# Two steps of mixing work in a row between the dense products of a hybrid encoder layer

## The chip, the cores and the metric

The kernel runs on one core of a Trainium2 chip. The metric is the device time of one execution in microseconds. The median of three runs of the kernel before is 2088.24 us (2086.25 to 2090.12).

## What is computed

One encoder layer with shared weights for two requests, a prompt of 512 tokens (`p`) and a sample of 1024 (`s`), all in float32 with a model width of 1024:

```
h    = rmsnorm(x)
proj = h @ w_in                       # 4096 columns: q, two gates, values, gate of HGRN; q, k, v of attention
o_h  = HGRN2 forward + HGRN2 backward # 4 heads of 128, gated linear recurrence, in chunks
o_a  = neighbourhood attention        # 8 heads of 64 on a grid 64 wide, windows of 8 x 16
x    = x + concat(o_h, o_a) @ w_out
x    = x + (silu(rmsnorm(x) @ w_gate) * (rmsnorm(x) @ w_up)) @ w_down
```

## The kernel before

The dense products (input projection, output projection, FFN) are made on TensorE from operands split into a high and a low part, three products for each block (lines 167 to 169 and 180 to 182, line 922 in the last stages). Each weight block is loaded by SyncE's queue, cast by ScalarE (line 109) and its rest taken by VectorE (line 110).

The mixing (HGRN and attention, and the norms) is written as Python generators, each cut into *steps* by `yield`. A step gives a few instructions to each engine. `queue` holds generators that wait, `active` those that have begun, up to a window. `micro()` takes one step of the active generator whose turn it is. Between the dense products stand calls of `quantum()`: one after every six dense matmuls. It adds `rate` to a credit, and takes one step for each whole credit. So the rate sets how densely mixing is strewn into dense work; `finish()` takes what is left at the end of a stage.

The list of units at the end of `trunk` sets the order of the work around the change:

- the prompt's first projections, with the norms as mixing (rate 1.8, window 2), up to some 80 us;
- the prompt's HGRN heads (rate 0.75, window 2), up to about 252 us;
- the sample's first projections with the prompt's attention as mixing (rate 1.8, window 6), up to about 430 us;
- the sample's HGRN heads (rate 0.75, window 2), up to about 757 us;
- the prompt's output projection and gate and up products, with the sample's attention as mixing (rate 1.8, window 4), up to about 1188 us;
- then the sample's output projection and FFN, without such mixing.

An HGRN head's work on one half of 512 tokens is `half_mix`: a step that makes the tiles (no TensorE work), one of block products of queries with key sums (`blocks`, line 311: eight matmuls, 16 in the profile's count, into PSUM tiles of 64 x 64), seven steps of levels, then the transposes of the keys (line 372) and the state products (line 379). A level makes eight block products from `kh` and `QQ` (line 311), scales the keys (line 330, VectorE) and copies them in another order (line 299, ScalarE), and rewrites both halves of `QQ` (lines 339 and 342, VectorE) for the next level. So a level can begin only when VectorE has rewritten `QQ` behind the block products of the level before. `out_half` then has three steps: output products (line 446), norm on VectorE, transposes (line 462).

The code is not the last word on the order. The framework's scheduler takes the instructions with the program's order as their priority, and sets each engine's order by when it holds the inputs of an instruction to be ready, and by when buffers are free.

Of the kernel before, what the change touches and what calls it, by code (L numbers as in the profile page):

```python
# [46 lines left out]
def trunk(ctx, tc, x_p, x_s, nmw, w_in, lbw, gnw, qnw, knw, rpb, w_out, nfw, w_g, w_u, w_d,  # L47
# [106 lines left out]
    def mm_nat(xT, ts, ws, done):  # L154


        pss = {}
        for s, slot in enumerate(ws):
            w = slot.rearrange("p h (k c) -> p h k c", k=2)
            for t in ts:  # L160
                if s == 0:
                    pss[t] = dense_ps()
                ps = pss[t]
                for j in range(2):
                    k = 2 * s + j
                    xh, xl = (xT[t // 4][i][:, k, t % 4 * 128:t % 4 * 128 + 128] for i in range(2))
                    pe.matmul(ps, lhsT=xh, rhs=w[:, 0, j, :], start=k == 0, stop=False)  # L167
                    pe.matmul(ps, lhsT=xh, rhs=w[:, 1, j, :], start=False, stop=False)  # L168
                    pe.matmul(ps, lhsT=xl, rhs=w[:, 0, j, :], start=False, stop=k == NK - 1)  # L169
                if s == len(ws) - 1:  # L170
                    done(t, ps)
                quantum()

    def mm_tr(ps, xT, w, t0=0, n=512):

        wv = w.rearrange("p h (k c) -> p h k c", k=NK)
        ts = slice(t0, t0 + n)
        for k in range(NK):
            xh, xl = xT[0][:, k, ts], xT[1][:, k, ts]
            pe.matmul(ps[:, ts], lhsT=wv[:, 0, k, :], rhs=xh, start=k == 0, stop=False)  # L180
            pe.matmul(ps[:, ts], lhsT=wv[:, 0, k, :], rhs=xl, start=False, stop=False)  # L181
            pe.matmul(ps[:, ts], lhsT=wv[:, 1, k, :], rhs=xh, start=False, stop=k == NK - 1)  # L182
            if k % 2 == 1:
                quantum()
# [3 lines left out]
    mix = {"rate": 0.0, "credit": 0.0, "window": 2}  # L188
    active, queue = [], []

    def micro():
        while True:
            while queue and len(active) < mix["window"] and queue[0][0]():
                active.append(queue.pop(0)[1]())
            if not active:
                return False
            g = active.pop(0)
            try:
                next(g)
            except StopIteration:  # L200
                continue
            active.append(g)
            return True

    def quantum():
        mix["credit"] += mix["rate"]
        while mix["credit"] >= 1:
            mix["credit"] -= 1
            if not micro():
                mix["credit"] = 0  # L210

    norms = {}

# [1067 lines left out]
```

## Time and profile before

| what | value |
| --- | --- |
| median of three runs | 2088.24 us |
| the profiled execution, its time | 2091.29 us |
| its span, first to last instruction | 2089.5 us |
| busy: TensorE, its weight loads | 1996.0 us, 1598.9 us |
| busy: VectorE, ScalarE, GpSimd | 1231.8 us, 812.1 us, 379.9 us |
| mean granted TensorE clock | 0.984 |

Busy time is the union of an engine's instructions. Ends of matmuls are modelled, and matmuls overlap, so a row of the timeline that says 0.39 us doesn't mean that the next cannot start for so long: the distance between starts is what counts. In a timeline, "PE" is TensorE's matmuls, "PEld" its weight loads, "DVE" VectorE, "ACT" ScalarE; a row may hold several instructions (xN).

### The profile page before, as it was taken

The page shows a single profiled execution, that of the slowest core. Times are in us where ns is not written, and L with a number is a line of the kernel's source. Part 1 is how long each engine was busy: PE and PEld are TensorE (multiplying, and loading weights), DVE is VectorE, ACT ScalarE, POOL GpSimd, SP SyncE. Part 2 cuts the span into 40 slices and gives each one's busy share as a digit, 9 for nine tenths or more (in the row PEclk, how much of TensorE's full clock was granted, in tenths as well). Part 3 has the DMA queues.
Part 4 walks back from the last instruction along what each step waited for, and adds up shares of the span by engine and source line. Part 5 has one row for each costly group of instructions (what it writes and reads, how often), then busy time and mean ns, then how long its engine had stood idle before and what let it go on. Part 6 is the DMA issues. An engine that isn't in the chain of part 4 may idle for free. (4 is left out here: it accounts for less than half of the span.)

```text
span 2089.5 us, 28456 instructions
## 1 busy us (share of the span) xinstructions
PE 1996.0 (96%) x10546; PEld 1598.9 (77%) x10546; DVE 1231.8 (59%) x2489; ACT 812.1 (39%) x1457; POOL 379.9 (18%) x310
## 2 busy tenths in 40 slices
PE   7999999999999999999999895899999998999999
PEld 5777887778788877778778784677777776887887
DVE  7677534576766667665654237656556554556644
ACT  5545335543433445555552224233223222323332
POOL 1200000000000000011112103344444441244300
PEclk9999999999999999999999997899999999999999
DMA  7832463432122274444455521223232224755443
GB/s 229 258 102 76 128 207 108 132 92 86 41 72 86 61 225 138 115 137 136 133 156 165 211 76 35 72 100 96 91 116 96 91 94 144 253 172 176 139 138 117
DMA packets 236833, 266.54 MB, mean 128 GB/s; under 512 B 19653, under 2 KB 168155, under 8 KB 236439
## 3 DMA queue, kind: packets, MB, share of 16 engines
q1 hardware_dynamic: 191904, 192.59, 30.8%
q10 hardware_dynamic: 41079, 61.27, 8.3%
q0 software_dynamic: 3712, 10.87, 1.7%
q8 instruction: 83, 1.36, 0.3%
q14 instruction: 55, 0.45, 0.1%
HBM read 194.84 MB, written 70.20 MB: 127 GB/s over the span
## 5 line engine op out<-in xcount | busy, mean ns | idle before, releaser
L110 DVE TENSOR_TENSOR w<-wst,w 128x1024 fp32r<-128x1024 f32 x128 | 157.1, 1229 | 147.9 <-ACT w L109 147.4
L109 ACT CAST w<-wst 128x1024 fp32r<-128x1024 f32 x128 | 134.1, 1048 | 175.2 <-PE pd L169 71.0
L922 PE MATMUL pd<-bo,ao 128*128 128x512 f32 x792 | 194.5, 393 | 4.6 <-ACT bo L916 4.6
L922 PEld LDWEIGHTS pd<-bo,ao 128*128 128x128 f32 x792 | 150.1, 190 | 36.6 <-ACT bo L916 5.0
L922 PE MATMUL pd<-opA,w 128*128 128x512 f32 x528 | 135.8, 400 | 18.0 <-ACT s L1036 10.8
L922 PE MATMUL pm<-bo,ao 128*128 128x512 f32 x594 | 147.9, 390 | 3.7 <-DVE bo L917 3.7
L922 PE MATMUL pd<-opS,w 128*128 128x512 f32 x528 | 135.9, 407 | 14.2 <-ACT opS L916 5.8
L182 PE MATMUL pd<-h2p,w 128*128 128x512 f32 (+1 forms) x368 | 143.0, 389 | 0.0
L180 PE MATMUL pd<-h2p,w 128*128 128x512 f32 (+1 forms) x368 | 142.5, 387 | 0.0
L181 PE MATMUL pd<-h2p,w 128*128 128x512 f32 (+1 forms) x368 | 142.1, 386 | 0.0
L922 PE MATMUL pm<-opS,w 128*128 128x512 f32 x528 | 135.4, 399 | 5.9 <-DVE sg L1018 4.7
L922 PEld LDWEIGHTS pd<-opA,w 128*128 128x128 f32 x528 | 99.1, 191 | 45.9 <-ACT s L1036 17.3
L922 PEld LDWEIGHTS pd<-opS,w 128*128 128x128 f32 x528 | 100.4, 194 | 43.1 <-DVE u L1044 11.4
L922 PEld LDWEIGHTS pm<-bo,ao 128*128 128x128 f32 x594 | 111.3, 188 | 27.9 <-DVE bo L917 5.0
L167 PE MATMUL pd<-w,hs 128*128 128x512 f32 x320 | 130.9, 409 | 0.0
L916 ACT CAST w<-wst 128x512 fp32r<-128x512 f32 x110 | 64.7, 617 | 166.0 <-POOL S L909 82.4
L169 PE MATMUL pd<-w,hs 128*128 128x512 f32 x320 | 126.4, 395 | 0.0
L168 PE MATMUL pd<-w,hs 128*128 128x512 f32 x320 | 126.0, 394 | 0.0
L922 PEld LDWEIGHTS pm<-opS,w 128*128 128x128 f32 x528 | 99.8, 192 | 32.1 <-DVE sg L1018 8.1
L917 DVE TENSOR_TENSOR w<-wst,w 128x512 fp32r<-128x512 f32 x110 | 89.3, 829 | 57.4 <-ACT w L916 57.3
L811 POOL DMA_DIRECT2D ost<-ot_p x8 | 4.3, 540 | 649.5 <-DMA pj_s<-ev 637.1
L917 DVE TENSOR_TENSOR ao<-wst,ao 128x768 fp32r<-128x768 f32 x77 | 88.6, 1155 | 8.4 <-ACT ao L916 6.8
(233 smaller groups left out, 4320.0 us busy)
## 6 DMA issues: line engine op xcount, KB each, us to landing
wst<-in_w_in_dram SPq DMA_DIRECT2D x68, 512.0 KB, 4.3
wst<-in_w_gate_dram SPq DMA_DIRECT2D x44, 512.0 KB, 3.9
wst<-in_w_up_dram SPq DMA_DIRECT2D x44, 512.0 KB, 4.3
wst<-g_S SPq DMA_DIRECT2D x44, 384.0 KB, 3.2
wst<-g_A SPq DMA_DIRECT2D x33, 384.0 KB, 3.7
g_S<-S ACTq DMA_DIRECT2D x44, 256.0 KB, 2.4
pj_s<-ev ACTq DMA_DIRECT2D x40, 256.0 KB, 2.4
bias<-bias_d SPq DMA_DIRECT2D x192, 48.0 KB, 2.0
```

The lines of the kernel that those rows point to most:

```text
L109: act.copy(out=w[:, 0, :], in_=s)
L110: dve.tensor_tensor(out=w[:, 1, :], in0=s, in1=f32(w[:, 0, :]), op=ALU.subtract)
L167: pe.matmul(ps, lhsT=xh, rhs=w[:, 0, j, :], start=k == 0, stop=False)
L168: pe.matmul(ps, lhsT=xh, rhs=w[:, 1, j, :], start=False, stop=False)
L169: pe.matmul(ps, lhsT=xl, rhs=w[:, 0, j, :], start=False, stop=k == NK - 1)
L180: pe.matmul(ps[:, ts], lhsT=wv[:, 0, k, :], rhs=xh, start=k == 0, stop=False)
L181: pe.matmul(ps[:, ts], lhsT=wv[:, 0, k, :], rhs=xl, start=False, stop=False)
L182: pe.matmul(ps[:, ts], lhsT=wv[:, 1, k, :], rhs=xh, start=False, stop=k == NK - 1)
L811: st.dma_start(out=s, in_=dram[b, "o", k][:, u * 512:u * 512 + 512])
L916: act.copy(out=dst[0], in_=src)
L917: dve.tensor_tensor(out=dst[1], in0=src, in1=f32(dst[0]), op=ALU.subtract)
L922: pe.matmul(ps, lhsT=l[a], rhs=r[b_], start=start and i == 0, stop=stop and i == 2, skip_group_check=more)
```

## The change

`quantum()` now does nothing until the credit has reached two, and then takes steps until less than one is left.

```diff
     def quantum():
         mix["credit"] += mix["rate"]
-        while mix["credit"] >= 1:
-            mix["credit"] -= 1
-            if not micro():
-                mix["credit"] = 0
+        if mix["credit"] >= 2:
+            while mix["credit"] >= 1:
+                mix["credit"] -= 1
+                if not micro():
+                    mix["credit"] = 0
```

Behind this place the changed program's lines have numbers higher by one: line 311 is 312 there, 372 is 373, 379 is 380.

How the order on TensorE moves is seen best in the sample's HGRN stretch. The first place is the end of the first half of the first head, where the second half begins. `KK` are the keys that are transposed, `q,ks` is the second half's first block product, `w,hs` are dense products. Before:

```order
L168 MATMUL pd<-w,hs_2564 128x512
L169 MATMUL pd<-w,hs_2565 128x512
L372 MATMUL pm<-ident,KK 128x128 x7
L167 MATMUL pd<-w,hs_2564 128x512
L168 MATMUL pd<-w,hs_2564 128x512
```

After the change:

```order
L168 MATMUL pd<-w,hs_2564 128x512
L169 MATMUL pd<-w,hs_2565 128x512
L373 MATMUL pm<-ident,KK 128x128 x7
L312 MATMUL pm<-q,ks 64x64 x8
L167 MATMUL pd<-w,hs_2564 128x512
L168 MATMUL pd<-w,hs_2564 128x512
```

Here two steps of different halves stand side by side; before, the block products came 24 dense products later, with the state products (L379) between.

The second place is a little further on, in the levels of that second half: two consecutive levels with the dense products between them. Before:

```order
L311 MATMUL pm<-QQ,kh 64x64 x8
L167 MATMUL pd<-w,hs_2564 128x512
L168 MATMUL pd<-w,hs_2564 128x512
L169 MATMUL pd<-w,hs_2565 128x512
L167 MATMUL pd<-w,hs_2564 128x512
L168 MATMUL pd<-w,hs_2564 128x512
L169 MATMUL pd<-w,hs_2565 128x512
L311 MATMUL pm<-QQ,kh 64x64 x8
```

After the change:

```order
L312 MATMUL pm<-QQ,kh 64x64 x8
L167 MATMUL pd<-w,hs_2564 128x512
L168 MATMUL pd<-w,hs_2564 128x512
L169 MATMUL pd<-w,hs_2565 128x512
L167 MATMUL pd<-w,hs_2564 128x512
L312 MATMUL pm<-QQ,kh 64x64 x8
L168 MATMUL pd<-w,hs_2564 128x512
L169 MATMUL pd<-w,hs_2565 128x512
```

The two levels are one pair in the changed program, but they don't stand side by side on TensorE: four dense products are between them, and then eight more follow up to the next pair.

## Rows read from the trace of the kernel before

**Rows 1.** The page's busy time of the engines.
```profile
PE 1996.0 (96%) x10546; PEld 1598.9 (77%) x10546; DVE 1231.8 (59%) x2489; ACT 812.1 (39%) x1457; POOL 379.9 (18%) x310
```
**Rows 2.** Busy time by stretch (start:end, length), its columns in the first line.
```profile
core 0: us, PE busy (x) PEld busy (x) DVE busy (x) ACT busy (x) POOL busy (x), PEclk, DMA share, GB/s
96.00:252.00 156.00, 155.62 (x1158) 123.40 (x1158) 112.69 (x269) 71.36 (x118) 0.00 (x0) 1.00 0.31 94
252.00:430.00 178.00, 177.70 (x889) 141.13 (x888) 79.80 (x235) 83.80 (x175) 0.00 (x0) 1.00 0.52 160
430.00:757.00 327.00, 326.08 (x2400) 259.99 (x2399) 221.38 (x556) 138.04 (x232) 6.38 (x10) 1.00 0.26 80
757.00:1188.00 431.00, 420.92 (x2161) 339.99 (x2160) 249.38 (x544) 196.15 (x369) 61.52 (x72) 0.99 0.52 155
```
**Rows 3.** Timeline of TensorE's matmuls (start, duration, what) around a block product.
```profile
459.92 0.39 PE L169 MATMUL pd<-w,hs 128*128 128x512 f32 x1
460.24 0.69 PE L311 MATMUL pm<-q,ks 128*64 128x64 f32 x16
460.86 0.50 PE L167 MATMUL pd<-w,hs 128*128 128x512 f32 x1
461.19 0.39 PE L168 MATMUL pd<-w,hs 128*128 128x512 f32 x1
461.42 0.40 PE L169 MATMUL pd<-w,hs 128*128 128x512 f32 x1
```
**Rows 4.** The same view around transposes of keys.
```profile
452.06 0.39 PE L169 MATMUL pd<-w,hs 128*128 128x512 f32 x1
452.29 0.93 PE L372 MATMUL pm<-ident,KK 128*128 128x128 f32 x7
452.97 0.48 PE L167 MATMUL pd<-w,hs 128*128 128x512 f32 x1
453.29 0.40 PE L168 MATMUL pd<-w,hs 128*128 128x512 f32 x1
```
**Rows 5.** All waits of TensorE's matmuls, 96 to 252 us (total, times, longest).
```profile
PE pm L462 <- DVE on L456: 0.2, 1, 0.2
```
**Rows 6.** Waits of TensorE's matmuls, 720 to 1188 us, the four largest.
```profile
PE pm L532 <- DVE dd L527: 4.5, 3, 2.3
PE pm L602 <- DVE nsm L124: 2.8, 1, 2.8
PE pm L602 <- DVE pr L598: 2.2, 6, 0.7
PE pm L462 <- DVE on L456: 0.9, 1, 0.9
```
**Rows 7.** Timeline of TensorE's matmuls where two block products stand together.
```profile
180.43 0.69 PE L311 MATMUL pm<-q,ks 128*64 128x64 f32 x16
180.94 0.84 PE L311 MATMUL pm<-QQ,kh 128*64 128x64 f32 x16
181.71 0.50 PE L181 MATMUL pd<-hp,w 128*128 128x512 f32 x1
```
**Rows 8.** Timeline of TensorE and VectorE where four dense products stand between levels.
```profile
683.59 0.69 PE L311 MATMUL pm<-QQ,kh 128*64 128x64 f32 x16
...
684.33 0.43 DVE L339 TENSOR_TENSOR QQ<-QQ,nt 128x256 f32<-128x256 f32 x1 [0.52 <-PE pm L311]
684.67 0.42 DVE L342 TENSOR_TENSOR QQ<-QQ,nt 128x256 f32<-128x256 f32 x1
...
685.33 0.69 PE L311 MATMUL pm<-QQ,kh 128*64 128x64 f32 x16
```
**Rows 9.** Line 339 by itself: its forms with their counts, and what VectorE waited for.
```profile
L339 DVE TENSOR_TENSOR QQ<-QQ,nt x72: 417/426/428, 107.8 to 716.0; 128x256 f32<-128x256 f32 x72
L339 DVE TENSOR_TENSOR QQ<-QQ,F x12: 426/426/429, 104.2 to 699.7; 128x256 f32<-128x256 f32 x12
  PE pm L311: 37.1, 52
```
**Rows 10.** Groups by line: VectorE's weight split (busy us, mean ns of one).
```profile
L110 DVE TENSOR_TENSOR w<-wst,w 128x1024 fp32r<-128x1024 f32 x128 | 157.1, 1229 | 147.9 <-ACT w L109 147.4
```

## The prediction

> **What bounds the kernel now.** I began with the busy time of the engines: TensorE is busy for 96% of the span [rows 1], so the first question was where it is not. Busy time by stretch answers it [rows 2]: from 96 to 757 us, which holds both stretches of HGRN mixing (rate 0.75) and the first stretch of attention mixing (rate 1.8), TensorE is busy for 659.4 of 661 us and the granted clock is 1.00. From 757 to 1188 us (the second attention mixing) it is busy for 420.9 of 431 us. A busy TensorE is not one at its peak, so I then read its timeline instruction by instruction. Dense products start 0.23 us apart. A step of eight 64-column block products (16 records of L311) begins 0.32 us after the dense product ahead of it, 0.09 late, and the first dense product behind it holds the engine for 0.33 us, 0.10 more than its fellows [rows 3]. A piece of 128-column transposes (L372) begins on time, and also costs 0.09 us behind it [rows 4]. So where TensorE is full, a change of the order of work can win two things: these switches, 0.19 us for a piece of L311 and 0.09 for another kind, and waits, of which the HGRN stretches have nearly none (0.2 us in all from 96 to 252 us [rows 5]). From the end of the sample's HGRN stretch through the second attention stretch (720 to 1188 us) four kinds of waits at the mixing's matmuls add up to 10.4 us, all for VectorE [rows 6].
>
> **What the change does to the order.** At rate 0.75 the steps that four quanta take go from 0, 1, 1, 1 to, over eight quanta, 0, 0, 2, 0, 0, 2, 0, 2: the same six. The prompt's four halves have 11 + 3 steps each, the sample's eight halves as many, so 56 and 112 places in the program become 28 and 56. At rate 1.8 five quanta go from 1, 2, 2, 2, 2 to 0, 3, 2, 2, 2: one step moves on by one quantum, 6 dense products. No step, transfer or byte is added or lost. But TensorE doesn't get this order: the framework's scheduler places an instruction where it holds its inputs to be ready. In an HGRN stretch mostly one half is in work, so both steps of a pair are levels of the same half, and the second needs the query tile that VectorE rewrites (L339, L342) behind the first. The order shows what is left: counting uninterrupted pieces of mixing matmuls between dense ones, the prompt's HGRN stretch goes from 51 to 44 and the sample's from 96 to 89. Where the two steps belong to different halves, or are independent, they do join (the first place above); where they are levels of one half the second is put four dense products later, and then eight or fourteen follow where six and twelve stood in turn (the second place). In the attention stretches the pieces go from 44 to 43 and stay at 83.
>
> **The cost, part by part.**
> - Switches saved. Of the 14 pieces that vanish in the HGRN stretches, 12 began with L311: 12 x 0.09 = 1.1 us. 11 ended with L311: 11 x 0.10 = 1.1 us. 3 ended otherwise: 3 x 0.09 = 0.3 us. Together 2.5 us at most. In ten of the joined pieces an L311 now stands right behind a 128-column step, and no row shows whether it still starts 0.09 late there; if it does, 0.9 us is lost again, 1.6 us are left. The one place where two L311 steps already stand side by side runs through without a gap: the second starts 0.51 us behind the first, sooner than the dense product behind a single one did (0.62) [rows 3, 7]; but both are 64 columns wide. I take the middle, 2.0 us.
> - A rule on these switches. Rows 4 show 0.09 us lost behind a piece that changes nothing in the width of the array's columns. The Trainium skill's page TensorEngine Tiling (Array Packing), section Key Properties, says that changing the tiling mode drains the engine. By that rule alone what counts is how often 64-column work begins, and L311 stands alone in 95 runs before and 96 after: the gain would be nil instead of 2.0 us. Rows 3 agree with it at the entry; rows 4 show that it isn't the whole price, so I stay with the rows.
> - The attention stretches. One piece fewer of 127: 0.2 us.
> - The closer follower. L311 behind L311 with five dense products or fewer between stood 11 times and stands 22 times now, 19 of them at exactly four. The trace has one such pair at four whose second depends on the first [rows 8]: the first starts at 683.59 us, VectorE has rewritten the tile by 685.09, and the second starts at 685.33, exactly where 0.23 us a product puts it. So four products cover the chain with 0.24 us over, if VectorE is free when the first ends. It waited for TensorE at L339 in 52 of 84 cases, 0.7 us on average [rows 9]; in the other 32 it was the later one. If 32/84 of the 19 close pairs find it late, that is seven. One can be late by anything from nothing to one weight split (L110, 1.23 us [rows 10]); half of that less the 0.24 is 0.4 us, so 2.8 us. The pair of rows 8 and the six that stand at five lost nothing, so I take half, 1.4 us; the ends are 0 and 19 x (1.23 - 0.24) = 19 us.
> - VectorE, ScalarE and the queues. The same instructions stand in another order. SyncE's loads of v and hg for HGRN and of bias and vb for attention move past weight loads by some places. The weights are loaded two units ahead, 24 quanta or more of 1.4 us for a pair of head units, and the DMA engines are at 26 to 52% in these stretches [rows 2]: covered, so nothing; without the cover a weight load would be late by its own few us once.
> - Stretches behind 1188 us and ahead of 96 us hold the same order on TensorE up to pieces of norm transposes: nothing.
>
> The sum is -2.0 - 0.2 + 1.4 = -0.8 us. The profiled execution took 2091.29 us and would take 2090.5; the median of the runs before, 2088.24, lies 3.05 below it, so the forecast for the median is 2087.4 us. What a measurement of this kernel can tell from no change is about 0.2%, 4.2 us: **the same**.
>
> **The rivals.**
> - *It is slower because the pairs wait.* TensorE takes its matmuls in order, so when the second L311 of a pair waits, eight or fourteen dense products stand behind it that need nothing from it. If VectorE is behind by a whole weight split at half of the 19 close pairs, TensorE loses 9.5 x 0.99 = 9.4 us, the sum is +7.2, the time 2095.4 us. It decides from 6.4 us of waits on, 0.34 us at each of the 19. For it speaks that VectorE is busy for 221 of 327 us in the sample's stretch [rows 2], and that a slot in VectorE's queue is fixed; against it, that eleven close places of before lost next to nothing. The Trainium skill's page Perfetto Trace Analysis, section Optimization Strategy, counsels interleaving regimes with different limits; by it, coarser interleaving is this rival. 0.19.
> - *It is faster because the attention waits shrink.* The 10.4 us of rows 6 hang on single instructions of VectorE at the start of each head pair and of the norms. The step that moves on by a quantum gives these 1.4 us more. If half of them went, 5.2 us, the sum would be -6.0 and the time 2082.2 us. For it speaks that a 1.67 us wait is of that size; against it, that the order of pieces there hardly differs (83 and 83), and a wait can as well move as vanish. 0.22.
> - *It does what its words say.* If pairs ran as one piece, some 73 of 147 pieces would go, 73 x 0.19 = 13.9 us, and the time would be some 2074 us. The order of the changed program speaks against it: 133 pieces are left. 0.02.
>
> **How the numbers follow.** The forecast has 0.57, the two faster cases 0.24, the slower one 0.19. These are also the chances of faster and slower by over 0.2% and of the same. The range reaches from just below the faster case, 2081.0, to 2093.5, where waits of 7.5 us at the pairs are still inside; what lies beyond is the upper part of the slower rival, the words-come-true case and the lower part of the faster one.
>
> **What would show it right or wrong.** In the profile of the changed kernel the switches should read as in rows 3 and 4; both HGRN stretches should keep TensorE busy for over 99%, and each end 1 us or so earlier against their start; L311 behind L372 tells the 0.09 that I could not price. Waits of TensorE named L311 with a VectorE line L339 or L342 (one line further down there), over 6 us in all, would show the slower rival. The list of waits from 720 to 1188 us, much shorter than 10.4 us, would show the faster one. The prediction is wrong if the HGRN stretches gain more than 5 us, or if the difference comes from behind 1188 us, where I see no change.

## The result, and the profile after

The changed kernel is **slower**: 2099.56 us (median of four runs, 2099.26 to 2100.14) where the kernel before took 2087.3 us in the runs beside it; the ratio is 1.0057, with a 95% interval from 1.0039 to 1.0074. The prediction was 2087.4 us, no change. The profiled execution took 2099.26 us, with a span of 2097.4 us, 7.9 us more than before's profile.

The sums on the page hardly move [rows 1]; TensorE is busy for 2.4 us more:

```profile
PE 1998.4 (95%) x10546; PEld 1600.9 (76%) x10546; DVE 1232.4 (59%) x2489; ACT 811.7 (39%) x1457; POOL 382.2 (18%) x310
```

By stretch [rows 2], the two with attention mixing (252 to 430 us and 757 to 1188 us) lose most, 3.1 and 4.5 us of busy time, and the two with HGRN mixing lose 1.0 and 1.6:

```profile
96.00:252.00 156.00, 154.58 (x1154) 122.95 (x1153) 114.00 (x269) 70.23 (x117) 0.00 (x0) 1.00 0.32 95
252.00:430.00 178.00, 174.61 (x863) 137.99 (x862) 77.49 (x230) 80.09 (x169) 0.00 (x0) 0.99 0.49 151
430.00:757.00 327.00, 324.52 (x2400) 260.01 (x2399) 220.32 (x552) 138.46 (x234) 6.41 (x10) 1.00 0.25 77
757.00:1188.00 431.00, 416.39 (x2135) 334.80 (x2135) 253.18 (x548) 197.59 (x371) 60.34 (x69) 0.99 0.53 151
```

The waits of TensorE's matmuls (total, times, longest). From 96 to 252 us, against 0.2 us in [rows 5]:

```profile
PE pm L312 <- DVE QQ L343: 0.8, 1, 0.8
PE pm L463 <- DVE on L457: 0.5, 2, 0.3
```

From 430 to 757 us, where the kernel before has 0.9 us, all for `on`:

```profile
PE pm L463 <- DVE on L457: 1.5, 2, 1.2
PE pm L380 <- ACT Kn L374: 0.9, 2, 0.8
```

From 252 to 430 us, where the kernel before has none:

```profile
PE pm L533 <- DVE dd L528: 2.8, 2, 2.0
PE pm L603 <- DVE pr L599: 0.3, 1, 0.3
```

From 720 to 1188 us, against [rows 6]:

```profile
PE pm L603 <- DVE s L598: 5.3, 2, 3.1
PE pm L533 <- DVE dd L528: 4.7, 4, 2.3
PE pm L603 <- DVE pr L599: 2.7, 7, 0.6
PE pm L463 <- DVE on L457: 1.5, 2, 1.2
PE pd L167 <- ACT ev L245: 0.7, 1, 0.7
```

`on` is the normed output of an HGRN head, `Kn` ScalarE's copy of the transposed keys, `dd` the scaled query or key tile of an attention head pair, `pr` and `s` the scores and their sums in the softmax, `nsm` a small tile of a norm, `ev` the copy of a dense product out of PSUM. The wait that the slower rival was built on (L312 for `QQ`) occurs once, for 0.8 us. All the same the time is lost, and in stretches for which I had written 0.2 us of gain.

Fixed times can't be compared where everything shifts. So I counted TensorE's dense products, of which every kernel has the same number, and took the time from product 240 to 768 (the prompt's HGRN stretch), 768 to 1248 (the prompt's attention), 1248 to 2304 (the sample's HGRN) and 2304 to 3216 (most of the sample's attention) from the starts in the two timelines. Two pieces are read by themselves: products 984 to 1032, where the prompt's second head pair begins, and 2448 to 2520, around the first gate unit, ahead of which the norms must be done. Before's profile has 167.6, 141.6, 349.6 and 324.9 us, and 17.1 and 37.7 us for the pieces. The table gives the difference to these in every kernel's profile, and the ratio of its runs to those of the kernel before beside them (95% interval).

| run | ratio | HGRN p | attn p | HGRN s | attn s | 984-1032 | 2448-2520 |
| --- | --- | --- | --- | --- | --- | --- | --- |
| the change | 1.0057 (1.0039-1.0074) | +0.8 | +4.8 | +1.1 | +5.7 | +4.2 | +3.5 |
| x1 pairs, both | 1.0050 (1.0036-1.0064) | +0.7 | +3.6 | +1.7 | +7.7 | +3.2 | +5.2 |
| x2 attn p alone | 1.0008 (0.9995-1.0021) | 0.0 | +0.1 | +2.5 | -0.5 | 0.0 | +1.3 |
| x3 attn s alone | 0.9994 (0.9983-1.0004) | 0.0 | +0.3 | +0.4 | +1.2 | 0.0 | +0.3 |
| x4 norms alone | 0.9997 (0.9988-1.0007) | 0.0 | +0.2 | -0.2 | +3.3 | 0.0 | +0.7 |
| x5 pairs, p | 1.0026 (1.0013-1.0039) | +0.8 | +3.6 | +1.3 | +2.1 | +3.1 | -0.4 |
| x6 pairs, s | 1.0026 (1.0015-1.0036) | 0.0 | 0.0 | +0.6 | +5.3 | 0.0 | +4.9 |
| x7 ends single | 1.0019 (1.0008-1.0030) | +0.1 | +1.5 | +1.1 | +4.8 | +1.4 | +2.8 |
| x8 end of s paired | 1.0033 (1.0021-1.0045) | +0.1 | +0.7 | +2.6 | +5.8 | 0.0 | +6.0 |
| x13 pairs s, 0.8 | 1.0006 (0.9994-1.0018) | 0.0 | 0.0 | +0.5 | +2.5 | 0.0 | +0.2 |
| x14 pairs, 0.8 | 1.0044 (1.0028-1.0060) | -0.1 | +2.0 | +1.1 | +2.0 | +2.2 | +0.7 |
| x15 before, 0.8 | 0.9995 (0.9986-1.0004) | 0.0 | +0.1 | +1.8 | -0.6 | 0.0 | +2.6 |
| x16 x5, weights on POOL | 1.0011 (1.0002-1.0019) | 0.0 | +0.2 | +1.3 | +1.5 | -0.2 | +0.2 |
| x17 both mends | 1.0007 (0.9997-1.0017) | 0.0 | +1.6 | +2.5 | -0.2 | -0.3 | 0.0 |
| x18 x14 again | 1.0042 (1.0027-1.0057) | 0.0 | +8.8 | +2.8 | -0.5 | +2.2 | 0.0 |

Two things are to be kept in mind with these differences. They hold more than waits: where the order has moved, other mixing matmuls stand in a stretch or a piece. From 984 to 1032 the change, x1, x5 and x7 have eight transposes of `dd` more than before, an estimated 0.9 us by the starts in the timeline of the change. x14 and x18 have 18 mixing matmuls more there and no wait of TensorE, and get the time back behind the piece (-2.7 us from 1032 to 1248), so their +2.2 is no loss. From 2448 to 2520 the kernel before, the change, x1, x5 and x6 all have 134 mixing matmuls, of the same kinds. And the four stretches of the change add up to 12.4 us, where the span grew by 7.9: ahead of product 240 and behind 3216 its profile is 1.5 and 3.0 us shorter. The part behind 3216 is also 3.0 to 4.1 us shorter in x2, x15 and x17 and no shorter in x4 and x13, all of which measure like before, so that it differs from run to run.

How far one profile can be trusted stands in the table too: x4 and x5 have TensorE's order of before in the sample's attention stretch, and read +3.3 and +2.1 there, most of it at its entry; in the piece from 2448 to 2520 they read +0.7 and -0.4. The two pieces are the steadier measure. A profile is of one run, and x5's is of the shortest of its six, 4.3 us under their median.

### The profile page after: what moved, and what is told of

It is laid out like the page before. It is cut to its first block, busy times and chain, and to the rows that moved or that the text cites. A ratio compares the mean times of both kernels' runs of the same rounds, so it can differ in the third digit from the quotient of the medians.

```text
span 2097.4 us, 28437 instructions
## 1 busy us (share of the span) xinstructions
PE 1998.4 (95%) x10546; PEld 1600.9 (76%) x10546; DVE 1232.4 (59%) x2489; ACT 811.7 (39%) x1457; POOL 382.2 (18%) x310
```

## The experiments

**Which stretch's edit does it.** Four kernels change `quantum()` in some stretches only. The threshold is two where the condition holds, and one (the code of before) elsewhere:

```diff
-        if mix["credit"] >= 2:
+        if mix["credit"] >= (2 if mix["rate"] < 1 else 1):      # x1
+        if mix["credit"] >= (2 if mix["window"] == 6 else 1):   # x2
+        if mix["credit"] >= (2 if mix["window"] == 4 else 1):   # x3
+        if mix["credit"] >= (2 if mix["window"] == 2 and mix["rate"] > 1 else 1):  # x4
```

> The change acts at rate 0.75 alone (both HGRN stretches); the attention and norm stretches are as before. The attention theory (the loss sits in the two stretches at rate 1.8 with six and four jobs in work, where steps come in threes) expects 2086 to 2090 us, the time of before, with both HGRN stretches within 1.5 us of before and the clock at 1.00 in the first attention stretch. The pairs theory (the loss comes from pairs of HGRN steps that wait) expects 2096 to 2100 us.

> The change acts in the prompt's attention stretch alone (rate 1.8, six jobs). The attention theory expects 2091 to 2093 us: the 4.8 us that this stretch lost, with a wait of TensorE for the tile dd of about 2 us and a fall of the clock behind it. The pairs theory expects before's time, 2086 to 2089 us.

> The change acts in the sample's attention stretch alone (rate 1.8, four jobs). The attention theory expects 2091 to 2094 us: the 5.5 us that this stretch lost, with two waits for s of 2 to 3 us near the start. The pairs theory expects before's time, 2086 to 2089 us.

> The change acts in the first stretch alone (the prompt's and sample's norms, rate 1.8, two jobs in work). Both theories expect little: the two traces differ there by 1.6 us in favour of the change, so 2085 to 2088 us; if the changed order of the norms shifted everything behind it, the time would lie above 2090 us.

x1 took 2101.98 us beside 2091.17 of the kernel before: it has the whole loss, and x2, x3 and x4 have none (2091.79, 2090.88, 2091.10 us). So the attention theory fell as I had written it: the steps that come in threes at rate 1.8 cost nothing. But the pairs theory did not win either. The table puts x1's loss into the attention stretches, +3.6 and +7.7 us, whose own steps it does not pair, and x1's waits from 755 to 1100 us are those of the change:

```profile
PE pm L603 <- DVE s L598: 5.3, 2, 3.1
PE pm L533 <- DVE dd L528: 4.6, 4, 2.2
```

The HGRN pairs are paid for behind their own stretch. The order shows how that is possible. In the sample's HGRN stretch the transposes of the last half (L462) end at dense product 2262 before, and at 2272 in x1; the first attention matmuls follow at 2354 and 2360, the first transposes of softmax rows at 2460 and 2471. The attention's pool of tiles is opened where HGRN's is closed. I call this the tail theory: the pairs let the last half end later, and the attention steps stand six to eleven dense products later against the dense work.

**Where the pairs must stand to cost.** In x5 and x6 `set_mix` gets a threshold of two for one HGRN stretch alone. In x7 it holds for the first 76 quanta of the prompt's and the first 150 of the sample's HGRN stretch, in x8 only behind quantum 150 of the sample's.

```diff
-        while mix["credit"] >= 1:
+        if mix["credit"] >= mix["least"]:   # x5, x6: least=2 by set_mix
+            while mix["credit"] >= 1:
...
+        mix["pairs"] -= 1                   # x7: set_mix(0.75, 2, 76) and (0.75, 2, 150)
+        if mix["credit"] >= (2 if mix["pairs"] >= 0 else 1):
...
+        if mix["credit"] >= (2 if mix["pairs"] < 0 and mix["rate"] < 1 else 1):  # x8
```

> Pairs in the prompt's HGRN stretch alone. The profiles so far put the loss of the HGRN pairs behind their own stretches, in the attention stretch that follows each. The tail theory (the pairs end the last half of the stretch some ten dense products later, so the attention that follows runs later against the dense products) expects 3 to 5 us over before, nearly all of it in the prompt's attention stretch, and the sample's attention stretch as before, since TensorE's order there is that of before. The theory that pairs wait where they stand expects 0 to 2 us.

> Pairs in the sample's HGRN stretch alone. The tail theory expects 6 to 9 us over before: the prompt's attention stretch as before, the sample's HGRN stretch within 2 us of before, the sample's attention stretch 5 to 8 us longer, with two waits of TensorE for s of 2 to 3 us just ahead of the first gate unit. The theory that pairs wait where they stand expects under 3 us, in the HGRN stretch.

> Pairs in both HGRN stretches except their ends: the last 20 quanta of the prompt's and the last 26 of the sample's go by single steps as before. The tail theory expects the time of before within 3 us: the order puts the first attention matmuls of the sample back at dense product 2354, where before has them (2360 with pairs throughout). The theory that the pairs themselves cost expects 8 to 12 us over before, as with pairs throughout.

> The complement, at one place: pairs only in the last 26 quanta of the sample's HGRN stretch (8 pairs), everything else as before. The tail theory expects nearly the whole loss of the sample's attention stretch, 5 to 8 us over before, with the two waits for s. The theory that the pairs themselves cost expects under 1 us over before.

x5 stands 6.1 us over before (2097.04 to 2090.98), x6 4.8 us (2095.77), and the two ratios together make x1's. Each loses in the attention stretch that follows it, and x5 loses 3.1 of its 3.6 us there in the piece from 984 to 1032 (a wait is 2.0 us of it, the transposes that moved in some 0.9 us), where x6 has nothing. x8 is the plainest: eight pairs at the end of one stretch cost 6.3 us (2097.24), as much as all the pairs of x6. x7 was to be within 3 us, and was 3.9 us over (2094.89, 1.0008 to 1.0030): without the ends most of the loss is gone but not all. Its order has the attention back at product 2354, and it still loses 2.8 us at the gate unit, with a 3.3 us wait for `pr`, and has 2.1 us of waits in the prompt's attention stretch. In x2 the first softmax transposes stand six products later than before (2466), for 1.3 us at the gate unit and no loss in the whole. So lateness alone does not decide; presumably, and not shown, it is which steps meet at that place.

What is lost around the gate unit is seen in TensorE's timeline. Before, two waits stand there, the longer one put down to a norm's instruction on VectorE:

```profile
815.36 0.52 PE L602 MATMUL pm<-ident,pr 128*128 128x128 f32 x3 [2.76 <-DVE nsm L124]
816.36 0.47 PE L602 MATMUL pm<-ident,pr 128*128 128x128 f32 x1 [0.49 <-DVE pr L598]
```

In x6 (lines three higher) there are two for the softmax itself, the second 9 us behind the first:

```profile
815.74 1.51 PE L605 MATMUL pm<-ident,pr 128*128 128x128 f32 x6 [2.13 <-DVE s L600]
824.82 1.36 PE L605 MATMUL pm<-ident,pr 128*128 128x128 f32 x6 [3.14 <-DVE s L600]
```

Scores, softmax on VectorE and ScalarE, and transposes depend on each other. In before's order one more round has its scores (L589) at product 2485, with eleven dense products behind them; in x6 they have come to stand behind product 2496, where the gate unit's first product needs the norms and nothing dense is left to put between.

**The prompt's piece: a queue.** At product 1008 or so, 317.75 us, TensorE waits 1.98 us for `dd` in the changed kernel. `dd` comes from `raw`, a load on SyncE's queue. Before, each of the second pair's two `raw` loads goes out ahead of a weight load (L108), which stands in the queue until one of two staging buffers is free:

```profile
284.65 0.43 SPq L495 DMA_DIRECT2D raw<-pj_p  x1
...
290.81 0.39 SPq L108 DMA_DIRECT2D wst<-in_w_in_dram  x1
...
299.72 0.43 SPq L495 DMA_DIRECT2D raw<-pj_p  x1
...
304.71 0.39 SPq L108 DMA_DIRECT2D wst<-in_w_in_dram  x1
```

In the changed kernel each goes out behind it, 6.7 and 6.2 us later:

```profile
290.94 0.39 SPq L108 DMA_DIRECT2D wst<-in_w_in_dram  x1
291.38 0.47 SPq L496 DMA_DIRECT2D raw<-pj_p  x1
...
305.45 0.39 SPq L108 DMA_DIRECT2D wst<-in_w_in_dram  x1
305.89 0.51 SPq L496 DMA_DIRECT2D raw<-pj_p  x1
```

x9 and x10 take the `raw` loads to another queue; x11 and x12 test another idea for the sample's stretch, that a higher rate would put independent steps between the rounds at the gate unit.

```diff
-                    ld.dma_start(out=r, ...)                         # x9 on x5, x10 on before
+                    (st if H == 1 else ld).dma_start(out=r, ...)
-                    set_mix(1.8, 4))                                 # x11 on the change, x12 on before
+                    set_mix(2.25, 4))
```

> As the run with pairs in the prompt's HGRN stretch alone, but the prompt's loads of raw go out on POOL's queue, which is idle there, instead of SyncE's, where they had come to stand behind weight loads that wait for a staging buffer. The queue theory (3.6 us of the prompt's attention stretch hang on raw loads issued late) expects the 2.0 us wait for dd gone and that stretch at 141.5 to 143.5 us instead of 145.2, the whole 2 to 4 us faster than with the pairs alone. The rival (the shift against the dense products costs it, whatever the queue) expects the stretch at 145 us again.

> The kernel before with the prompt's loads of raw on POOL's queue: the control of the run ahead of it. The queue theory expects the prompt's attention stretch within 1 us of before's 141.6 (its raw loads stand ahead of the weight loads already) and the time of before within 3 us. If this run gains as much as the one with pairs, the queue is a gain of its own and says nothing on the pairs.

> The changed kernel with rate 2.25 instead of 1.8 in the sample's attention stretch: ahead of the first gate unit TensorE's order then holds steps of the next head pair between those of the two that ran late. The cover theory (the stretch loses since the last pieces ahead of the gate unit have no independent work between their softmax steps) expects the waits for s there, 5.3 us, to fall below 3 us and the stretch at 325 to 329 us instead of 330.6. The rival (more mixing without dense products between costs more) expects it at 331 to 336 us.

> The kernel before with rate 2.25 in the sample's attention stretch: the control of the run ahead of it. The cover theory expects less to win than in the changed kernel, 0 to 3 us, since only 3.25 us of waits stand ahead of the gate unit here; the rival expects 1 to 5 us more than before.

All four came out worse than both ideas. x9 is 1.0046 (1.0032 to 1.0061) and x10, the control, 1.0038 (1.0025 to 1.0052), with the prompt's attention stretch at 150.5 and 155.2 us. 9.4 of x10's 13.5 us are lost by product 840, at the stretch's entry (some of the 13.5 is mixing done earlier; the next stretch is 4.0 us shorter). The POOL queue, with nothing ahead of them, sent the second pair's `raw` loads out at once, into DMA engines that were busy for 1.05 and 0.92 of the time from 265 to 275 us; ScalarE's square of one of them (L498) waited 8.63 us, and behind it in ScalarE's order stood the casts of keys and queries for which TensorE then waited 7.8 us:

```profile
275.27 0.63 ACT L498 ACTIVATE sq<-raw 128x512 f32<-128x512 f32 x1 [8.63 <-DMA raw<-pj_p]
275.92 0.58 ACT L544 CAST KS<-pm 64x512 fp32r<-64x512 f32 x1
```

So these two say nothing on the queue theory; a load that comes too early can hold an engine as one that comes late does. x11 and x12 are 1.0169 and 1.0125: a higher rate is no remedy. The sample's attention stretch grew by 38 and 31 us instead of shrinking (5.7 of the 38 are the change's own, and part of both is mixing done earlier; the whole grew by 35.5 and 26.0 us). Whether steps between the rounds would cover the waits at the gate unit is not settled by it: in x11 the waits for `s` there fell from 5.3 to 2.1 us, but 20 more mixing matmuls stand in that piece, with waits for `pr`. In x12, from 825 to 870 us, TensorE stood 9.5 us for one `dd`, and its clock was granted at 0.77, where the kernel before has 1.00:

```profile
825.00:870.00 45.00, 30.57 (x191) 26.17 (x191) 32.70 (x84) 21.93 (x44) 1.10 (x2) 0.77 0.29 79
```

**The two mends.** Now each stretch is put right while all the pairs stay. In x13, which is x6 with rate 0.8 in the sample's HGRN stretch, TensorE's order in the sample's attention stretch is again that of before, instruction for instruction. x14 has pairs in both stretches at 0.8, x15 is the control of x13 without pairs. x16 is x5 with the weights of the prompt's attention stretch on POOL's queue, and not the `raw` loads.

```diff
-    set_mix(0.75, 2, least=2)            # x13: sample's HGRN stretch; x14: both
+    set_mix(0.8, 2, least=2)
-    set_mix(0.75, 2)                     # x15
+    set_mix(0.8, 2)
-    w_nat(w_in, 512 * c)                 # x16: loads of these units by q
+    w_nat(w_in, 512 * c, st if b == "s" and c < 5 else ld)
```

> Pairs in the sample's HGRN stretch, as in the run with pairs there alone, but at rate 0.8 instead of 0.75, so that the stretch's last steps come sooner: TensorE's order in the sample's attention stretch is then that of before, instruction for instruction, while all the pairs stay. The tail theory (the pairs cost by the place at which they let the attention start) expects the loss of 5.3 us in that stretch gone, with a longest wait near the gate unit of 2.8 us for nsm as in before, and the whole within 2 us of before. The theory that the pairs themselves cost expects 4 to 6 us over before, as at 0.75.

> Pairs in both HGRN stretches at rate 0.8. SyncE's order then has both raw loads of the prompt's second head pair ahead of the weight loads again, as before has them, and the sample's attention stretch is in before's order. The tail theory expects the prompt's attention stretch at 141 to 143 us (145.2 with the pairs at 0.75), the sample's at 325 to 328 us, the whole within 3 us of before. The theory that the pairs themselves cost expects 9 to 12 us over before.

> The control: the kernel before with rate 0.8 in the sample's HGRN stretch and no pairs. Its order has the first attention matmuls at dense product 2337 and one softmax round less without dense products ahead of the gate unit. The tail theory expects before's time or 1 to 4 us less, the sample's attention stretch at 322 to 326 us. If it gains as much as the run with pairs at 0.8 gains on the one at 0.75, the rate is a gain of its own.

> Pairs in the prompt's HGRN stretch alone, and the weights of the first two units of the prompt's attention stretch (8 loads) go out on POOL's queue, so no raw load of the second head pair stands behind one of them on SyncE. The queue theory expects no wait for dd over 1 us at the second head pair (2.0 with the weights on SyncE) and the stretch at 141.5 to 143.5 us instead of 145.2. The rival, that the late start costs it whatever the queue, expects 144 to 146 us.

x13 is back: 1.0006, where x6 had 1.0026; +0.2 us at the gate unit, where x6 had +4.9. The two waits for `s` are gone and before's wait for `nsm` stands in their place:

```profile
PE pm L605 <- DVE nsm L124: 2.8, 1, 2.8
```

x15 shows that the rate by itself gains nothing (0.9995). x16 is at 1.0011 (1.0002 to 1.0019), where x5 had 1.0026, and the prompt's attention stretch is 0.2 us from before's. Its second `raw` load goes out at 297.54 us, and the 2.0 us wait is gone; this is all that TensorE waits there from 255 to 405 us:

```profile
PE pm L535 <- DVE dd L530: 0.4, 1, 0.4
```

The mend also took away a 0.8 us wait at the first pair and the 0.8 us of the HGRN stretch, so the queue is shown as the cause for the stretch as a whole, not for each wait. The intervals of x5 and x16 overlap, so by time alone this step is near the noise. No run has these weights on POOL's queue without pairs; the kernel before has no wait from 252 to 430 us that it could win there. Two runs with every load on SyncE's queue agree with the queue: in x14 and x7 the second `raw` load goes out at 298.00 and 299.37 us, ahead of the weight load, and the wait for `dd` at the second pair is 0.4 and 0.3 us.

x14 did not come out as expected: 1.0044 in time, with a profile that shows only 4 us. x17 has both mends on the pairs of both stretches (0.8 in the sample's alone), and x18 is x14 once more.

> Both mends together on pairs in both HGRN stretches: rate 0.8 in the sample's HGRN stretch, and the 8 weight loads of the prompt's attention stretch on POOL's queue. The tail and queue theories expect the prompt's attention stretch at 141 to 143 us, the sample's at 325 to 328 us, and the whole 0 to 4 us over before, where the same pairs without the mends stand 10 us over it. A cost of the pairs themselves that only showed elsewhere would leave 6 us or more.

> The run with pairs in both stretches at rate 0.8 once more: its runs spread from 2093 to 2104 us and its profile came from one of the fast ones, 4 us over before, with both attention stretches within 2.1 us of before. If the high ones are the kernel's own, a median of 2099 to 2102 us comes back and a profile of a slow one shows where; if not, the median lies at 2092 to 2096 us.

**x17 took 2093.10 us beside 2090.45, ratio 1.0007 (0.9997 to 1.0017).** All the pairs of both stretches are in it, and what is left of the loss can't be told from nothing (0.17% at most, where x1 has 0.50%). x18 came back at 1.0042, and this time the profile shows the place, the first products of the prompt's attention stretch. The hand-over moved once more: two loads of 2 MB (`hs`) and the stores of the last dense products meet there, the DMA engines are busy for 1.04 and 0.99 of the time from 262 to 272 us, and a copy out of PSUM must wait until the store of the copy two before it has landed:

```profile
264.46 0.59 ACT L247 COPY ev<-pd 128x512 f32<-128x512 f32 x1 [3.57 <-DMA pj_p<-ev]
...
269.86 0.59 ACT L247 COPY ev<-pd 128x512 f32<-128x512 f32 x1 [3.87 <-DMA pj_p<-ev]
```

TensorE needs that PSUM buffer for the next dense product:

```profile
265.10 0.50 PE L167 MATMUL pd<-w,hs 128*128 128x512 f32 x1 [0.43 <-ACT ev L247]
270.50 0.80 PE L167 MATMUL pd<-w,hs 128*128 128x512 f32 x1 [3.74 <-ACT ev L247]
```

In before's profile the DMA engines are as busy there (1.05 from 265 to 270 us), but its last copy for such a store stands at 261.52 us, 8 us sooner than x18's. x14's profile has 0.6 us of this wait, x18's 4.2 us: the same program, so the wait depends on how the transfers happen to fall. No run has rate 0.8 in the prompt's HGRN stretch without pairs, so it is not shown whether this loss is one of the pairs or of the rate. No version was measured as faster than the kernel before.

## Why the prediction was wrong

- **HGRN stretches: right.** They were to come out near nothing, -2.0 + 1.4 us. They read +0.8 and +1.1 us with the change, and in x17, which has all the pairs, no loss of the whole can be measured. That the sum came near is in part luck: the two terms were each mis-sized, and a third wait was not in it. *Closer follower*, 1.4 us: the waits named L312 for `QQ` are 0.8 us in all, so VectorE was nearly always in time. Not foreseen were 0.9 us at the state products (L380), which wait for ScalarE's copy `Kn`. *Switches saved*, 2.0 us: a joined piece with an L312 behind a 128-column step saves nothing. In the changed kernel's timeline

```profile
460.15 0.93 PE L373 MATMUL pm<-ident,KK 128*128 128x128 f32 x7
461.01 0.69 PE L312 MATMUL pm<-q,ks 128*64 128x64 f32 x16
461.62 0.50 PE L167 MATMUL pd<-w,hs 128*128 128x512 f32 x1
```

  the block product starts 0.86 us behind the transposes, where a dense product starts 0.68 behind them [rows 4]: 0.18 us, the exit price and the entry price together. I had left the entry open and counted the exit as saved. Of the ten joined pieces with an L312 behind, five are of this kind. The other five have the state products ahead, and cost more than the two steps apart. First the step alone, in the kernel before, then the joined piece:

```profile
455.82 1.72 PE L379 MATMUL pm<-v,Kn 128*128 128x128 f32 x14
457.30 0.47 PE L167 MATMUL pd<-w,hs 128*128 128x512 f32 x1
457.61 0.39 PE L168 MATMUL pd<-w,hs 128*128 128x512 f32 x1
```

```profile
465.84 1.72 PE L380 MATMUL pm<-v,Kn 128*128 128x128 f32 x14
467.49 0.88 PE L312 MATMUL pm<-QQ,kh 128*64 128x64 f32 x16
468.31 0.50 PE L167 MATMUL pd<-w,hs 128*128 128x512 f32 x1
```

  Apart, the state products take 1.48 us to the next start with 0.08 behind it, and an L311 0.09 + 0.62 + 0.10 [rows 3]: 2.37 us. Joined they take 1.65 + 0.82 + 0.10 = 2.57 us, 0.2 us more, so five of them lose some 1.0 us.

  The Trainium skill's page TensorEngine Tiling (Array Packing), section Key Properties, says that changing the tiling mode drains the engine. Read as a price at the start of 64-column work, as the prediction read it, this rule made the gain nil; I had weighed it and stayed with the rows of single pieces. The trace agrees with it so far as both seams have a price (0.18 and 0.17 us). It does not tell why the L312 behind the state products takes 0.2 us longer, and the exit price of rows 4 stays beside the rule.
- **"The attention stretches. One piece fewer of 127: 0.2 us": the step that failed.** In place of 0.2 us of gain these stretches read +4.8 and +5.7 us. The term counted pieces, and the count did hold (x2, x3: the edit there costs nothing). But it priced a stretch by its own edit alone. The stretch inherits the place at which the one ahead of it ends, and in the sample that moved by ten dense products. There the price stood at the gate unit (+3.5 us in the change, +4.9 in x6), where a softmax round had lost the dense products behind it. That the order is the cause is shown by x13, which has before's order and none of it; that it is the missing cover is read from the timeline and not tested by itself.
- **"VectorE, ScalarE and the queues … covered, so nothing": failed.** I asked whether a weight load would be late, and looked only at the loads of the HGRN stretches and their cover. What was late was a small load that now stood behind a weight load, and TensorE waited 1.98 us for what hung on it. A queue in which a load changes its place has to be read in both directions.
- **The slower rival came nearest the time, but not by its cause.** It gave 2095.4 us by waits of the pairs themselves on VectorE; those were 0.8 us. The test that I had written down told them apart at once: waits named L311 (now L312) of over 6 us did not come. **The faster rival** looked at the right waits [rows 6] with the wrong sign: the list from 720 to 1188 us did not shrink, it grew from 10.4 to 14.9 us: 5.3 us for `s` came, and 2.8 us for `nsm` went.
- The clock, which the prediction left at 1.00 for the first attention stretch: behind the 1.98 us wait it was granted at 0.96 and then 0.87 (1.00 before in both), which adds to the 4.2 us of that piece. It does not always come: x5 waits as long at the same place (2.0 us), keeps 1.00, and loses 3.1 us in the piece. First the change, then x5:

```profile
310.00:320.00 10.00, 8.02 (x40) 6.51 (x39) 6.96 (x20) 2.53 (x5) 0.00 (x0) 0.96 0.61 187
320.00:330.00 10.00, 10.00 (x48) 7.47 (x47) 5.35 (x19) 6.31 (x15) 0.00 (x0) 0.87 0.34 81
```

```profile
310.00:320.00 10.00, 8.00 (x41) 6.23 (x40) 7.11 (x22) 3.53 (x8) 0.00 (x0) 1.00 0.56 164
320.00:330.00 10.00, 10.00 (x56) 7.10 (x55) 5.09 (x21) 6.51 (x16) 0.00 (x0) 1.00 0.35 83
```

What stays open: why the order of x7, which starts the sample's attention where before does, still loses 2.8 us at the gate unit (x15, in another order, reads +2.6 there and is no slower in the whole); and how much of x14's and x18's loss stands at the entry in every run (7.6 of x18's 8.8 us in that stretch do).

## What to carry to other kernels

Where work is strewn between other work by a rate, price an edit at the hand-over too: when does the last step of the stretch end, and what starts only then. Look in each issuing queue for small loads that the edit moves behind one that waits for a buffer. And before a cause is believed, apply the edit to one stretch at a time, and read in which stretch the time is lost: here the two were different ones.

## What the runs showed of the hardware

- A load that needs nothing can be 6.2 us late because the entry ahead of it in its queue waits for a buffer (305.89 against 299.72 us). The Trainium skill's page Trainium Kernel Development and Optimization, section Key Constraints, says that issuing DMAs from several engines only saves the sequencer's issue time, since all run on the same DMA engines. x16 shows more than that: eight weight loads on POOL's queue took x5's 3.6 us in the prompt's attention stretch down to 0.2, in one profile each. x10 shows the other side, on DMA engines that were busy for 1.05 and 0.92 of the time: the loads on another queue held ScalarE for 8.63 us.
- 128-column transposes followed by 64-column products pay 0.18 us at the seam, as much as both pay with dense products between. 14 state products followed by 64-column products take 0.2 us more than the two apart.
- A wait of some microseconds on TensorE can be followed by a lower granted clock, and need not be. Behind 1.98 us the change was granted 0.87 for 10 us, x5 behind 2.0 us 1.00. Behind 3.74 us x18 was granted 0.50 from 270 to 275 us, which is the level of 1.2 GHz instead of 2.4, and its dense products started 0.43 us apart instead of 0.23.
